# Where accumulating DMAs and transposes stand in the order of a hybrid encoder layer

## The chip, the cores and the metric

The kernel runs on one core of a Trainium2 chip. The metric is the device time of one execution in microseconds (us). Most executions of a kernel agree within 0.3%. The core has five engines, each with its own queue of instructions that it works off in order: TensorE (PE, matmuls, with its weight loads shown apart as PEld), VectorE (DVE), ScalarE (ACT), GpSimd (POOL) and SyncE (SP), which issues most of the DMA transfers. An instruction waits on semaphores for what other engines or transfers must finish first, and what is queued behind it on its engine waits with it.

## The reference

One layer of an encoder with two parallel groups of heads, for 256 tokens of 2048 features, in fp32:

```python
hn = _rmsnorm(h, norm_w[i])
proj = hn @ w_in[i]
q, v, f_fwd, f_bwd, z_a, b_gate, c_gate, h_b, z_b = jnp.split(proj, IN_SPLITS, axis=-1)
o_a = _hgrn2_bidirectional(jax.nn.silu(q), v, f_fwd, f_bwd, lb_all[:, i])
o_a = _head_rmsnorm(o_a, hgrn_norm_w[i]) * jax.nn.silu(z_a)
y_b = b_gate * _short_conv(c_gate * h_b, conv_w[i])
o_b = _rmsnorm(y_b, conv_norm_w[i]) * jax.nn.silu(z_b)
h = h + jnp.concatenate([o_a, o_b], axis=-1) @ w_out[i]
gate = jax.nn.sigmoid(h @ w_ple_gate[i])
h = h + (p[i] @ w_ple[i]) * gate
```

and a last RMSNorm. `_hgrn2_bidirectional` is a gated linear recurrence over 16 heads of 128 features, worked in chunks of 64 tokens, forward and backward: within a chunk masked scores times `v`, and between chunks a state of 128 x 128 for each head.

## The kernel before

**Tiles and precision.** Every fp32 operand of a matmul is split in two fp32r parts, a high and a low one, and products are made of three partial matmuls. `xs` holds the split activations. Weights come in raw tiles of up to 1 MB (`raw`, three buffers), loaded by SP. ACT casts a part of a tile to the high half of a `spl` tile (L101), DVE subtracts to get the low half (L102), and PE reads `spl`. There are five `spl` buffers; the split of a part is issued three parts ahead of its use.

**Stages.** Group A has 16 heads, worked as 8 pairs in four blocks of two pairs, called block 0, 2, 4 and 6 after the first pair (`two_pairs(i)`). A block has, for each of its pairs e = 0 and 1, three gemms of 16 k tiles: forward forget gate (FF), backward forget gate (FB) and Q, lines L403 (short matmuls, 256 columns) and L405 (long ones, 512 columns). Then `v` and `z_a` of both pairs follow: in block 0 as two gemms, in blocks 2, 4 and 6 together in `gemm_vz` (through `half`, lines L525 to L527) over eight pairs of k tiles. For three of these, k pairs 2, 4 and 6, seven products are made in place of eight, from sums and differences of the weights' blocks. These sums are made in DRAM: `prepare` copies the blocks (L306, DMAs of SP, "vz<-in_w_in_dram"), `add_up` accumulates into them with DMAs of POOL in three steps (step 0 on L314, two DMAs a sum; steps 1 and 2 on L318, one each), and then the weights' stream loads the result ("raw<-vz"). `w_out` has 16 such tiles of sums, four sets of four, 48 steps of `add_up` in all, worked off one by one by `pump()` (DMAs "sums<-in_w_out_dram", "sums<-sums"). Group B follows, 8 times the gemms CG, HB, BG and ZB with a convolution, then the gemms of `w_out`, of the gate and of the embedding, and a last norm.

**Mixing.** Behind the three gemms of a pair, `mix_forgets` scales `xf` and `qt` by the tokens' norms on POOL (L470), takes sigmoids on ACT (L592, L594) and logarithms (L601). `mix_pair` does scans and exponentials on DVE and ACT and makes `kc`, `qc` (L689) and `kx` (L695) on POOL. `scores` are PE's products (L708) and the cross-chunk part `cx` (L752), in the PSUM buffer "x"; POOL writes the masked scores `s` (L757). `outputs` makes the heads' outputs. In the block after, `gate_two` gates (`zt`, POOL L616), `finish_two` normalizes (`ogz`, DVE L626), and `turn` transposes a pair's outputs on PE (L636), one pair into the PSUM buffer "y" and one into "x", from which ACT (L639) and DVE (L640) write the split `mixa`. So `cx` of a block's first pair, in `gemm_vz`, uses the buffer "x" that the transpose of the previous block's second pair filled before.

**What sets the order.** The program is written out with `at(dt, fn)`: `fn` is issued `dt` k tiles later (`tick()` counts them and runs what is due; `gemm_vz` has 49 of them, every other gemm of 2 MB 16). The instructions of an engine then run in the order of the queue, with some splits and evacuations at a higher priority. In block i before the change: the `prepare`s at 0, 8 and 16; the nine `add_up`s and four `pump`s from tick 24 on every 6; `mix_forgets` behind each Q; scores of the first pair 4 ticks into `gemm_vz`; scores of the second pair 28 ticks and its outputs 40 ticks behind the end of `gemm_vz`, in the next block. `rest()` of a block runs behind the Q of the next block's first pair: gates at once, `finish_two` 30 ticks on, the transposes at 36 and 42. A gemm's `orders` ("kicks", `ONE` and `BOTH`) turn round the order of short and long matmuls at one or two k tiles.

The functions that the change touches, and what calls them:

Of the kernel before, what the change touches and what calls it, by code (L numbers as in the profile page):

```python
# [115 lines left out]
def tile_hymba_encoder(  # L116
# [34 lines left out]

    VZ_SUMS = (2, 4, 6)
    dramp = ctx.enter_context(tc.tile_pool(name="dramp", bufs=1, space=bass.MemoryType.DRAM))
    vz_prepared = {}
    blocks = {}
    for i in range(0, 8, 2):
# [4 lines left out]
        if i:  # L161
            blocks[B_V, i], vz_prepared[i] = [], []
            for q in range(8):
                srcs = [
                    [w_in[c + i + b, q // 4, :, 2 * (q % 4) : 2 * (q % 4) + 2] for b in range(2)] for c in (B_V, B_ZA)
                ]
                if q in VZ_SUMS:
                    sums = dramp.tile([P, 4, 512], F32, name=f"vz{i}_{q}")
                    vz_prepared[i].append((srcs, sums))
                    blocks[B_V, i].append(ws.add_sums(*srcs, sums))  # L170
                else:
                    blocks[B_V, i].append(ws.add(*srcs[0], *srcs[1]))
            continue
# [156 lines left out]
    def tick():  # L330
        now[0] += 1
        if now[0] in range(120, 160, 10):
            prepare(prepared[(now[0] - 120) // 10])
        due = sorted(e for e in pend if e[0] <= now[0])
        for e in due:
            pend.remove(e)
        for e in due:
            e[2]()
# [95 lines left out]
    def gemm_vz(i, vt, zt):  # L434
# [8 lines left out]
        main = [[acc[m], acc[2 + m]] for m in range(2)]  # L443
        for q1, q5, q6, q7 in half(main, extra, range(8), VZ_SUMS, blocks[B_V, i], xs, xq[0], True):
            d = xq[1][:, 0]
# [339 lines left out]
    def two_pairs(i):  # L785
# [4 lines left out]
        before = last_two[0]  # L790
        if i:

            todo = vz_prepared[i]
            for z, what in enumerate(todo):
                at(8 * z, lambda what=what: prepare(what))
            turns = [lambda what=what, step=step: add_up(what, step) for step in range(3) for what in todo]
            for j in (3, 7, 11, 12):
                turns.insert(j, pump)
            for j, fn in enumerate(turns):
                at(24 + 6 * j, fn)  # L800
        if i == 2:
# [9 lines left out]
        for e in range(2):  # L811
# [3 lines left out]

            kick = {(0, 1): ({}, ONE, BOTH)}.get((i, e), (ONE, BOTH, {}) if e == 0 else ({}, {}, {}))
            for j, (c, dst) in enumerate(((B_FF, xf[:, 0]), (B_FB, xf[:, 1]), (B_Q, qt))):
# [32 lines left out]
        else:  # L850
# [4 lines left out]
            at(12, lambda: out(0))  # L855
            at(28, lambda: steps[1][0]())
            at(40, lambda: out(1))

        def rest():
            gate_two(i, zt)  # L860
            if i < 6:
                at(30, lambda: finish_two(ogs, ss, zt, ogs))
                for e in range(2):
                    at(36 + 6 * e, lambda e=e: turn(i + e, ogs[e], "yx"[e]))
            else:
# [26 lines left out]
    for i in range(8):  # L892
        cg = ctmp.tile([P, 2, T], F32, tag="cg", name=f"cg{i}", bufs=2)
        evac(gemm_in(B_CG, i, {} if i else ONE), lambda m: cg[:, m, :], ctmp)
        hb = ctmp.tile([P, 2, T], F32, tag="hb", name=f"hb{i}", bufs=2)
        evac(gemm_in(B_HB, i, {} if i else BOTH), lambda m: hb[:, m, :], ctmp)
        u = ub[i % 2]
        by_norms(cg, rbc2, 2)
        pool.tensor_tensor(out=u[:, :, 1 : T + 1], in0=cg, in1=hb, op=ALU.mult)
        pump()  # L900
        for m in range(2):
            ct = 2 * i + m
            dve.tensor_scalar(cg[:, m, :], u[:, m, 0:T], cvw[:, 0, ct : ct + 1], None, op0=ALU.mult)
            for j in (1, 2):
# [3 lines left out]
                )  # L908
        evac(gemm_in(B_BG, i), lambda m: hb[:, m, :], ctmp)
        pool.tensor_tensor(out=cg, in0=cg, in1=hb, op=ALU.mult)  # L910
# [322 lines left out]
```

## Time and profile before

| | us |
|---|---|
| median of 3 runs | 1167.51 |
| lowest, highest | 1163.05, 1168.25 |
| the profiled execution | 1164.41 |
| its span | 1162.7 |
| mean granted TensorE clock | 0.981 of full speed |

| engine | busy us | share of the span |
|---|---|---|
| PE | 1111.8 | 96% |
| PE's weight loads | 951.6 | 82% |
| DVE | 825.8 | 71% |
| ACT | 681.5 | 59% |
| POOL | 300.4 | 26% |

The DMA engines moved 286.42 MB, 63.5% of their time for the queue that SP's transfers use and 15.3% for that of the accumulating DMAs. In the profile a line names an instruction's line in the kernel, its engine, the tile that it writes and those that it reads, partitions x elements, and a count. Idle time stands in brackets with the engine and tile that ended it. An idle engine costs something only where another, or the end, waits for it.

### The profile page before, as it was taken

The numbers are of one execution on the slowest core, as the hardware profiler recorded it, in microseconds if no ns is written. First come the engines' busy times: TensorE is split into PE (matmuls) and PEld (weight loads), VectorE is DVE, ScalarE is ACT, GpSimd is POOL, SyncE is SP. The second block draws the span as 40 slices with busy tenths as digits, with TensorE's granted clock in tenths as the row PEclk, the third lists the DMA queues.
The fourth block names the chain that finished last, engine by engine and source line by source line (L and its number), as shares of the span: only waits on it lengthen the run. The fifth ranks groups of instructions, "written<-read, shape, count | busy, mean of one in ns | idle before, by whom it ended". The sixth has DMA issues, their size and how long they took to land.

```text
span 1162.7 us, 17008 instructions
## 1 busy us (share of the span) xinstructions
PE 1111.8 (96%) x6455; PEld 951.6 (82%) x6455; DVE 825.8 (71%) x1100; ACT 681.5 (59%) x948; POOL 300.4 (26%) x251
## 2 busy tenths in 40 slices
PE   9999998899959999499999999999999999999996
PEld 8888887678858888388888888888888888888886
DVE  7899485875848676576666687686567879878573
ACT  7786475755945577565644445444446655565563
POOL 1135226513352036322323223223222000000001
PEclk9999999899979999799999999999999999999999
DMA  9757977799576998676789989989776988887531
GB/s 346 296 194 261 322 223 159 215 328 267 192 173 223 340 285 227 161 269 207 195 250 292 287 227 268 329 230 269 213 211 214 335 284 283 314 286 283 199 127 73
DMA packets 86082, 286.42 MB, mean 246 GB/s; under 512 B 8304, under 2 KB 29424, under 8 KB 67312
## 3 DMA queue, kind: packets, MB, share of 16 engines
q1 hardware_dynamic: 69264, 258.76, 63.5%
q0 software_dynamic: 16448, 26.22, 15.3%
q8 instruction: 51, 0.84, 0.3%
q10 hardware_dynamic: 288, 0.34, 0.1%
q14 instruction: 31, 0.25, 0.1%
HBM read 283.20 MB, written 54.53 MB: 290 GB/s over the span
## 4 chain that ended last, share of the span: by engine, by line
PE 70%; DVE 8%; POOL 7%; ACT 7%; DMA 5%; issue 3%; SPq 0%; DVEq 0%; ACTq 0%; POOLq 0%
PE a L405 26%; PE a L403 13%; DVE spl L102 4%; DMA raw<-in_w_in_dram 3%; PE pg L995 3%; PE pg L994 3%; PE pg L993 3%; ACT spl L101 2%; DMA vz<-vz 2%; PE pa L525 2%; PE pa L527 2%; PE pa L526 2%; POOL kc L689 2%; PE avz L526 1%; PE avz L525 1%
## 5 line engine op out<-in xcount | busy, mean ns | idle before, releaser
L102 DVE TENSOR_TENSOR spl<-raw,spl 128x1024 fp32r<-128x1024 f32 (+2 forms) x419 | 500.1, 1209 | 238.7 <-ACT spl L101 236.6
L405 PE MATMUL a<-xs,spl 128*128 128x512 f32 x1792 | 623.8, 395 | 2.6 <-DVE vt L455 2.4
L101 ACT CAST spl<-raw 128x1024 fp32r<-128x1024 f32 (+2 forms) x419 | 412.5, 998 | 268.2 <-PE a L403 120.5
L403 PE MATMUL a<-xs,spl 128*128 128x256 f32 x1792 | 494.4, 278 | 0.0
L405 PEld LDWEIGHTS a<-xs,spl 128*128 128x128 f32 x1792 | 335.2, 188 | 80.4 <-issue 3.2
L403 PEld LDWEIGHTS a<-xs,spl 128*128 128x128 f32 x1792 | 336.2, 188 | 2.2 <-DVE spl L102 0.6
L1110 POOL TENSOR_TENSOR hh<-hh,fw 128x512 f32<-128x512 f32 (+1 forms) x9 | 10.9, 1224 | 251.5 <-ACT gt L1109 248.8
L465 ACT COPY r<-a 128x256 f32<-128x256 f32 x112 | 40.5, 369 | 48.9 <-PE a L403 48.8
L526 PE MATMUL avz<-spl,xs 128*128 128x512 f32 x138 | 56.6, 410 | 0.7 <-DVE spl L102 0.7
L525 PE MATMUL avz<-spl,xs 128*128 128x512 f32 x138 | 56.8, 411 | 0.0
L527 PE MATMUL avz<-spl,xs 128*128 128x512 f32 x138 | 55.7, 404 | 0.0
L752 PE MATMUL cx<-qc,kx 128*128 128x128 f32 x64 | 11.9, 344 | 37.5 <-DVE mixa L640 36.5
L470 POOL TENSOR_TENSOR xf<-xf,rbc 128x1024 f32<-128x1024 f32 x8 | 28.1, 3518 | 66.9 <-DVE rbc L381 49.1
L993 PE MATMUL pg<-spl,ht 128*128 128x512 f32 (+1 forms) x120 | 45.2, 377 | 0.0
L994 PE MATMUL pg<-spl,ht 128*128 128x512 f32 (+1 forms) x120 | 45.1, 376 | 0.0
L995 PE MATMUL pg<-spl,ht 128*128 128x512 f32 (+1 forms) x120 | 45.0, 375 | 0.0
L752 PEld LDWEIGHTS cx<-qc,kx 128*128 128x128 f32 x64 | 10.2, 242 | 38.1 <-issue 36.7
L689 POOL TENSOR_TENSOR kc<-dd,ge 128x256 f32<-128x256 f32 x16 | 33.2, 2072 | 29.0 <-DVE dd L680 16.5
L101 ACT CAST spl<-early 128x1024 fp32r<-128x1024 f32 (+1 forms) x29 | 28.7, 990 | 20.0 <-PE pb_y L527 7.5
L102 DVE TENSOR_TENSOR spl<-early,spl 128x1024 fp32r<-128x1024 f32 (+1 forms) x29 | 33.0, 1148 | 9.7 <-ACT spl L101 9.1
L592 ACT ACTIVATE xf<-xf 128x1024 f32<-128x1024 f32 x8 | 8.5, 1060 | 45.1 <-POOL xf L470 45.0
L525 PE MATMUL pa<-spl,mixa 128*128 128x512 f32 x88 | 34.5, 392 | 0.0
(322 smaller groups left out, 1725.8 us busy)
## 6 DMA issues: line engine op xcount, KB each, us to landing
raw<-in_w_in_dram SPq DMA_DIRECT2D x106, 1024.0 KB, 7.4
raw<-in_w_in_dram SPq DMA_DIRECT2D x82, 256.0 KB, 4.3
raw<-in_w_out_dram SPq DMA_DIRECT2D x36, 512.0 KB, 5.3
sums<-in_w_out_dram SPq DMA_DIRECT2D x32, 512.0 KB, 9.9
raw<-in_w_in_dram SPq DMA_DIRECT2D x26, 512.0 KB, 5.2
raw<-sums SPq DMA_DIRECT2D x13, 1024.0 KB, 5.0
vz<-in_w_in_dram SPq DMA_DIRECT2D x36, 256.0 KB, 9.6
raw<-vz SPq DMA_DIRECT2D x9, 1024.0 KB, 5.2
```

Source lines behind the costliest of these rows:

```text
L101: self.nc.scalar.copy(out=v[:, :, 0], in_=r)
L102: self.nc.vector.tensor_tensor(out=v[:, :, 1], in0=r, in1=v[:, :, 0], op=ALU.subtract)
L403: pe.matmul(a[:, :T], lhsT=lhsT, rhs=xs[:, kt, 0, :], start=False, stop=(kt == NKT - 1))
L405: pe.matmul(a, lhsT=lhsT, rhs=xs[:, kt, :, :].rearrange("p s n -> p (s n)"), start=(kt == 0), stop=False)
L465: act.copy(out=r, in_=acc[m][:, 1, :])
L525: pe.matmul(acc, lhsT=ah, rhs=w[:, 0], start=start, stop=False)
L526: pe.matmul(acc, lhsT=ah, rhs=w[:, 1], start=False, stop=False)
L527: pe.matmul(acc, lhsT=al, rhs=w[:, 0], start=False, stop=stop)
L689: pool.tensor_tensor(out=c64(dst[:, d]), in0=c64(src[:, d, :, half * P : (half + 1) * P]), in1=g.unsqueeze(3).broadcast_to([P, 2, 2, CH]), ...
L993: pe.matmul(acc[m], lhsT=lh, rhs=wh, start=(kt == 0), stop=False)
L994: pe.matmul(acc[m], lhsT=lh, rhs=wl, start=False, stop=False)
L995: pe.matmul(acc[m], lhsT=ll, rhs=wh, start=False, stop=(kt == nk - 1))
```

## The change

1. The sums of `v`'s and `z_a`'s weights for a block are made in the block before: `prepare` at ticks 50, 60, 70 of block i for block i + 2, `add_up` at the ticks below.
2. All steps for `w_out`'s sums are done in group B, six `pump`s in each of the eight rounds; the first set's `prepare`s go from block 0 to block 6.
3. `gemm_vz` takes its k pairs in the order 0, 1, 2, 3, 4, 6, 5, 7.
4. `finish_two` at tick 24, both transposes at tick 32, between FB and Q of the block's second pair; the second scores at 32, the second outputs at 42.
5. The kicks are put at other gemms.

```diff
-    VZ_SUMS = (2, 4, 6)
+    VZ_ORDER, VZ_SUMS = (0, 1, 2, 3, 4, 6, 5, 7), (2, 4, 6)
...
-            for q in range(8):
+            for q in VZ_ORDER:
...
     def tick():
         now[0] += 1
-        if now[0] in range(120, 160, 10):
-            prepare(prepared[(now[0] - 120) // 10])
...
-        for q1, q5, q6, q7 in half(main, extra, range(8), VZ_SUMS, blocks[B_V, i], xs, xq[0], True):
+        for q1, q5, q6, q7 in half(main, extra, VZ_ORDER, VZ_SUMS, blocks[B_V, i], xs, xq[0], True):
...
-        if i:
-
-            todo = vz_prepared[i]
+        if i == 6:
+            for z in range(4):
+                at(10 + 10 * z, lambda z=z: prepare(prepared[z]))
+        else:
+
+
+            todo = vz_prepared[i + 2]
             for z, what in enumerate(todo):
-                at(8 * z, lambda what=what: prepare(what))
-            turns = [lambda what=what, step=step: add_up(what, step) for step in range(3) for what in todo]
-            for j in (3, 7, 11, 12):
-                turns.insert(j, pump)
-            for j, fn in enumerate(turns):
-                at(24 + 6 * j, fn)
+                at(50 + 10 * z, lambda what=what: prepare(what))
+                for step in range(3):
+                    dt = (126 + 10 * z, 160 + 4 * z, 174 + 4 * z)[step] if i else 98 + 6 * step + z
+                    at(dt, lambda what=what, step=step: add_up(what, step))
...
-            kick = {(0, 1): ({}, ONE, BOTH)}.get((i, e), (ONE, BOTH, {}) if e == 0 else ({}, {}, {}))
+            kicks = {(0, 1): ({}, ONE, BOTH), (2, 0): (ONE, BOTH, {}), (4, 0): ({}, {}, BOTH), (6, 0): ({}, {}, BOTH)}
+            kick = kicks.get((i, e), ({}, {}, BOTH if i + e else {}))
...
-            at(28, lambda: steps[1][0]())
-            at(40, lambda: out(1))
+            at(32, lambda: steps[1][0]())
+            at(42, lambda: out(1))
...
-                at(30, lambda: finish_two(ogs, ss, zt, ogs))
+                at(24, lambda: finish_two(ogs, ss, zt, ogs))
                 for e in range(2):
-                    at(36 + 6 * e, lambda e=e: turn(i + e, ogs[e], "yx"[e]))
+                    at(32, lambda e=e: turn(i + e, ogs[e], "yx"[e]))
...
-        evac(gemm_in(B_CG, i, {} if i else ONE), lambda m: cg[:, m, :], ctmp)
+        evac(gemm_in(B_CG, i), lambda m: cg[:, m, :], ctmp)
...
-        evac(gemm_in(B_HB, i, {} if i else BOTH), lambda m: hb[:, m, :], ctmp)
+        evac(gemm_in(B_HB, i), lambda m: hb[:, m, :], ctmp)
...
         by_norms(cg, rbc2, 2)
+        pump()
...
-        evac(gemm_in(B_BG, i), lambda m: hb[:, m, :], ctmp)
+        evac(gemm_in(B_BG, i, {} if i else BOTH), lambda m: hb[:, m, :], ctmp)
```

How this moves instructions shows in the queues. The first place is POOL in block 2, from `kx` of the first pair to `xf` of the second (`vz_2`, `vz_4`, `vz_6` are the sums of the three k pairs, `sums_0_3` to `sums_0_5` tiles for `w_out`). Before:

```order
L695 TENSOR_TENSOR kx_1707<-kc_1701,ge_1688 128x512
L318 DMA vz_4_82<-vz_4_82 128x512
L318 DMA vz_6_83<-vz_6_83 128x512
L314 DMA sums_0_3_91<-in_w_out_dram 256x1x512
L318 DMA vz_2_81<-vz_2_81 128x512
L318 DMA vz_4_82<-vz_4_82 128x512
L318 DMA vz_6_83<-vz_6_83 128x512
L314 DMA sums_0_4_92<-in_w_out_dram 256x1x512
L314 DMA sums_0_5_93<-in_w_out_dram 256x1x512
L470 TENSOR_TENSOR xf_1709<-xf_1709,rbc 128x1024
```

And the same place in the changed kernel (lines count two less here), on through `gemm_vz`, with the next block's sums:

```order
L693 TENSOR_TENSOR kx_1703<-kc_1697,ge_1684 128x512
L468 TENSOR_TENSOR xf_1705<-xf_1705,rbc 128x1024
L468 TENSOR_TENSOR qt_1706<-qt_1706,rbc 128x512
L755 TENSOR_TENSOR s_2104<-early 128x256 x2
L314 DMA vz_2_84<-in_w_in_dram 256x1x256
L593 TENSOR_TENSOR qt_1706<-qt_1706,sq_2020 128x512
L314 DMA vz_2_84<-in_w_in_dram 256x1x256
L314 DMA vz_4_85<-in_w_in_dram 256x1x256 x2
L314 DMA vz_6_86<-in_w_in_dram 256x1x256 x2
L318 DMA vz_2_84<-vz_2_84 128x512
L318 DMA vz_4_85<-vz_4_85 128x512
```

The eight DMAs between `kx` and `xf` are gone from there; eight others now stand behind the first pair's `s`, within `gemm_vz`.

The second place is ACT in block 2, around the transposes' `mixa` of the previous block and the table load of the second pair's sigmoid (`spl65` to `spl67` are parts of weights). Before:

```order
L465 COPY r_1899<-a24_3_1_1802 128x256
L101 CAST spl65_1957<-raw32_1933 128x1024
L639 ACTIVATE mixa_499<-ogt0_1923,vec_108 128x256 x2
L101 CAST spl66_1991<-raw33_1986 128x1024
L639 ACTIVATE mixa_499<-ogt1_1968,vec_108 128x256
L592 ACT_TABLE_LOAD
L592 ACTIVATE xf3_1709<-xf3_1709 128x1024
L101 CAST spl67_2036<-raw33_1986 128x1024
L639 ACTIVATE mixa_499<-ogt1_1968,vec_108 128x256
```

And changed:

```order
L463 COPY r_1920<-a24_3_1_1804 128x256
L637 ACTIVATE mixa_499<-ogt0_1899,vec_108 128x256
L637 ACTIVATE mixa_499<-ogt1_1908,vec_108 128x256
L637 ACTIVATE mixa_499<-ogt0_1899,vec_108 128x256
L637 ACTIVATE mixa_499<-ogt1_1908,vec_108 128x256
L101 CAST spl65_1968<-raw32_1944 128x1024
L590 ACT_TABLE_LOAD
L590 ACTIVATE xf3_1705<-xf3_1705 128x1024
```

All four `mixa` now stand ahead of the table load and of a cast, where the last stood behind the sigmoid before.

The third place is POOL early in block 4, from `kx` of block 2's second pair to its `s`, in the changed kernel:

```order
L693 TENSOR_TENSOR kx_2476<-kc_2470,ge_2457 128x512
L687 TENSOR_TENSOR qc_2471<-pf_2447,ge_2457 128x256
L318 DMA vz_6_86<-vz_6_86 128x512
L318 DMA vz_2_84<-vz_2_84 128x512
L318 DMA vz_4_85<-vz_4_85 128x512
L318 DMA vz_6_86<-vz_6_86 128x512
L755 TENSOR_TENSOR s_2671<-early 128x256
L468 TENSOR_TENSOR xf_2401<-xf_2401,rbc 128x1024
L755 TENSOR_TENSOR s_2671<-early 128x256
```

The last four accumulating DMAs of block 4's sums stand there, ahead of `s`; before, the first two of the twelve (L314, `vz_2`) stood between this `kx` and `s`, and the others behind.

## The prediction

> **What bounds the kernel now.** I read the page's busy times first, then PE's waits, then the stretch ahead of the longest waits engine by engine, then the DMA.
>
> ```profile
> span 1162.7 us, 17008 instructions
> PE 1111.8 (96%) x6455; PEld 951.6 (82%) x6455; DVE 825.8 (71%) x1100; ACT 681.5 (59%) x948; POOL 300.4 (26%) x251
> L752 PE MATMUL cx<-qc,kx 128*128 128x128 f32 x64 | 11.9, 344 | 37.5 <-DVE mixa L640 36.5
> ```
>
> PE is busy for 96% of the span, so only three things shorten the kernel: PE's idle time, matmuls that run slowly, or fewer matmuls. The change leaves the matmuls as they are, so the first two are left. One line, `cx`, the first matmuls of a pair's scores, carries 37.5 us of idle time. PE's waits say how it is spread:
>
> ```profile
> PE cx L752 <- DVE mixa L640: 36.5, 3, 15.5
> PE a L405 <- DVE vt L455: 2.4, 2, 1.2
> PE avz L526 <- DVE spl L102: 0.7, 1, 0.7
> ```
>
> Three waits, the longest of 15.5 us, one in each of blocks 2, 4 and 6. `cx` takes the PSUM buffer "x", which the second transpose of the previous block filled and which DVE's `mixa` line frees. Why is `mixa` late? First POOL in block 4 (start, duration, instruction, idle time before it with its releaser), then ACT and PE:
>
> ```profile
> 322.70 1.05 POOL L695 TENSOR_TENSOR kx<-kc,ge 128x512 f32<-128x512 f32 x1
> 323.69 1.66 POOL L318 DMA_DIRECT2D vz<-vz  x2
> ...
> 328.82 0.81 POOL L318 DMA_DIRECT2D vz<-vz  x1 [1.80 <-DMA vz<-vz]
> 331.46 0.81 POOL L318 DMA_DIRECT2D vz<-vz  x1 [1.82 <-DMA vz<-vz]
> ...
> 333.05 3.26 POOL L470 TENSOR_TENSOR xf<-xf,rbc 128x1024 f32<-128x1024 f32 x1
> ```
>
> ```profile
> 324.07 1.28 ACT L592 ACT_TABLE_LOAD   x1
> 336.34 1.06 ACT L592 ACTIVATE xf<-xf 128x1024 f32<-128x1024 f32 x1 [10.98 <-POOL xf L470]
> 338.24 0.47 ACT L639 ACTIVATE mixa<-ogt,vec 128x256 fp32r<-128x256 f32 x1
> 341.99 0.48 ACT L639 ACTIVATE mixa<-ogt,vec 128x256 fp32r<-128x256 f32 x1
> ```
>
> ```profile
> 323.08 0.60 PE L636 MATMUL ogt<-ident,ogz 128*128 128x128 f32 x4
> 344.01 2.05 PE L752 MATMUL cx<-qc,kx 128*128 128x128 f32 x8 [12.10 <-DVE mixa L640]
> ```
>
> The chain reads backwards. POOL has `kx` done at 323.75. Its queue then holds accumulating DMAs, several of which wait for an earlier one to land, so `xf` starts only at 333.05. ACT sits 10.98 us on `xf`'s sigmoid with its table loaded, and behind it in its queue stand the second transpose's two `mixa`. PE did that transpose at 323.08, but ACT copies it out at 338.24 and 341.99, DVE's `mixa` line follows, and PE has stood for 12.10 us when `cx` starts.
>
> The stall also slows what follows it. PEclk, the seventh column here (after the busy times of five engines and before DMA share and GB/s), is the granted clock in the 6 us from each `cx`:
>
> ```profile
> 208.25:214.25 6.00, 6.00 (x20) 5.10 (x21) 5.58 (x10) 5.92 (x8) 2.52 (x3) 0.56 1.03 327
> 344.01:350.01 6.00, 6.00 (x18) 5.13 (x19) 6.00 (x8) 3.06 (x4) 4.24 (x4) 0.50 0.12 43
> 480.65:486.65 6.00, 6.00 (x18) 5.13 (x19) 6.00 (x8) 3.05 (x4) 4.23 (x4) 0.50 0.20 73
> ```
>
> Lost there: 6.00 x (0.44 + 0.50 + 0.50) = 8.6 us.
>
> **The change, part by part.** The sum is made against the profiled execution, 1164.4 us (span 1162.7 and 1.7 around it); the median of the runs shown, 1167.5, lies 3.1 above it. I don't add those 3.1, since the landing times in the stalls are a likely part of what varies.
>
> *The stall.* Behind block 4's `kx` POOL's order now has `xf` and `qt` at once: no accumulating DMA stands between. By the rows, `xf` can start at 323.75 instead of 333.05 and end by 327.0. On ACT all four `mixa` now stand ahead of the table load and the sigmoid, and both transposes are issued together at the end of FB, 16 k tiles of Q ahead of `v`/`z_a`. So the buffer is free long before `cx` asks for it: all 36.5 us go, and the 8.6 with them. What could be late next is the transposes' own input, which PE would wait for ahead of Q:
>
> ```profile
> 314.33 0.61 DVE L626 SCALAR_TENSOR_TENSOR ogz<-ogz,ss,zt 128x128 f32<-128x128 f32 x2
> ...
> 449.20 0.61 DVE L626 SCALAR_TENSOR_TENSOR ogz<-ogz,ss,zt 128x128 f32<-128x128 f32 x2
> ```
> ```profile
> 315.70 0.39 PE L405 MATMUL a<-xs,spl 128*128 128x512 f32 x1
> 318.48 0.60 PE L636 MATMUL ogt<-ident,ogz 128*128 128x128 f32 x4
> ...
> 451.67 0.60 PE L636 MATMUL ogt<-ident,ogz 128*128 128x128 f32 x4
> ```
>
> In block 4 `ogz` is complete at 314.94 and Q begins at 315.70, so it would be in time by 0.8 us. In block 6 it is complete at 449.81; Q begins 2.8 us (318.48 - 315.70) ahead of the transpose, at 448.9, so PE would wait 0.9 us. The gating's start moves six k tiles earlier, but in the rows `ogz` is paced by POOL's and ACT's gates, so I don't count that as a gain: +1.0 for block 6, bounds 0 and 3 (1 us in each block).
>
> *Order of the sums in `v`/`z_a`* (the sum for k pair 6 ahead of plain pair 5). The DVE work on the last sum no longer stands at the very end, where `a <- vt` waited 2.4 us: -2.0, bounds -2.4 and 0. Against it, four loads now follow one another faster. Block 4 shows how little slack there is now:
>
> ```profile
> 367.31 3.47 ACT L101 CAST spl<-raw 128x1024 fp32r<-128x1024 f32 x4 [2.52 <-DMA raw<-in_w_in_dram]
> ```
> ```profile
> 368.39 4.14 DVE L102 TENSOR_TENSOR spl<-raw,spl 128x1024 fp32r<-128x1024 f32 x4 [1.30 <-ACT spl L101]
> ```
> ```profile
> 371.02 0.39 PE L525 MATMUL avz<-spl,xs 128*128 128x512 f32 x1
> ```
>
> ACT already waits for the DMA there. The first of the four splits ends near 369.6 (368.39 and some 1.2), PE uses it at 371.02: 1.4 us to spare.
>
> *The accumulating DMAs.* Those of the next block's sums are now issued within `v`/`z_a` and early in the block after. What this does to the weight loads shows where the old order let them meet (issue, engine, operation, count, KB each, median us to landing; the first fence 190 to 216 us, with adds in flight, the second 360 to 370 us, without):
>
> ```profile
> vz<-vz POOLq DMA_DIRECT2D x5, 256.0 KB, 7.6
> raw<-vz SPq DMA_DIRECT2D x1, 1024.0 KB, 9.1
> raw<-in_w_in_dram SPq DMA_DIRECT2D x4, 256.0 KB, 6.8
> ```
> ```profile
> raw<-in_w_in_dram SPq DMA_DIRECT2D x6, 256.0 KB, 4.3
> raw<-vz SPq DMA_DIRECT2D x1, 1024.0 KB, 5.2
> ```
>
> A load of sums is 3.9 us later (9.1 against 5.2), a piece of plain weights 2.5 (6.8 against 4.3). With 1.4 us to spare, a load hit makes PE late by 1.1 to 2.5 us. Blocks 2 and 4 issue adds within `v`/`z_a`; block 6 does not. Bounds for a block: 0 (adds land in the plain first half), and 11.4 with all four late loads hit (2 x 2.5 + 2 x 3.9 - 1.4). I take one hit a block, 2 us, as the adds are spread by POOL's own work: +4.0 for the two, 0 to 23. [...]
>
> *`w_out`'s sums.* Twelve of 48 add-up steps go from group A to group B:
>
> ```profile
> 560.00:960.00 400.00, 400.00 (x2216) 346.54 (x2215) 278.91 (x372) 208.35 (x278) 97.03 (x82) 1.00 0.87 261
> q0 software_dynamic: 16448, 26.22, 15.3%
> ```
>
> In group B PE has no gap, while the DMA engines have 13% of 400 us free, 52 us. The adds' queue took 15.3% of 1162.7 us for 26.22 MB, 6.8 us per MB; 12 steps of 0.5 MB, 41 us, fit. Cost 0. [...]
>
> *Kicks* (which of the short and long matmuls of a k tile comes first, in other gemms than before) and the scores' and outputs' ticks move 4 and 2 k tiles, with the same instructions. The order within a pair of matmuls can move a gemm by little; 0, bounds -2 and +2, my estimate from the pace of a gemm, 24 of its long matmuls in 8.40 us in one order and 25 in another:
>
> ```profile
> 277.65:286.05 8.40, 8.40 (x24) 4.46 (x24) 1.00 0.85 186
> 300.00:308.40 8.40, 8.40 (x25) 4.58 (x25) 1.00 0.47 165
> ```
>
> **Sum:** 1164.4 - 36.5 - 8.6 - 2.0 + 4.0 + 1.0 = **1122.3 us**.
>
> **Rivals.**
>
> *The weights become the wait.* The two sums side by side need their loads in quick succession while adds share the DMA engines. For it: 1.4 us to spare, and 9.1 against 5.2. Against it: PE waited for splits 0.7 us in all so far, and an add is in flight for only part of the gemm. Three of four late loads hit: 2.5 + 2.5 + 3.9 - 1.4 = 7.5 a block, 15 for two, in place of the 4.0: 1122.3 - 4.0 + 15 = 1133 (1126 to 1140).
>
> *Only part of the stall goes.* Four `mixa` now come together on ACT and DVE; if DVE's queue of splits holds them up, `cx` waits again, or Q waits for "y" and "x". For it: DVE is busy in 5.58 to 6.00 of 6 us in the windows above. Against it: 16 k tiles of Q lie between. With half of the 45.1 us left: 1122.3 + 22.5 = 1145.
>
> *Slower: the adds hold up the second scores.* POOL's order puts four accumulating DMAs between `kx` of a block's second pair and the copy `s` that its outputs wait for, the later ones waiting for the earlier to land.
>
> ```profile
> 233.17 1.05 POOL L695 TENSOR_TENSOR kx<-kc,ge 128x512 f32<-128x512 f32 x1
> 277.17 2.51 POOL L757 TENSOR_TENSOR s<-early 128x256 f32<-128x256 f32 x2 [21.76 <-DVE early L756]
> vz<-vz POOLq DMA_DIRECT2D x1, 256.0 KB, 18.1
> ```
>
> From 234.2 to 277.2 there are 43 us for them. At the usual 7.6 us four in a row take 30. At the longest landing of the trace, 18.1 us, they take 72, so `s` comes 29 us late and PE stops at the outputs, in two places: 58, against the 47.1 gained (36.5 + 8.6 + 2.0): 1164.4 + 58 - 47.1 = 1175. It decides where a landing takes more than 43 / 4 = 10.8 us throughout. Against it: only single ones took that long, and three sums let the adds overlap.
>
> **How the numbers follow.** Forecast 1122.3 with its own range 1112 to 1130: 0.62. Weights, 1133: 0.25. Part of the stall, 1145: 0.08. Slower, 1175: 0.03; about no change, as where two of these meet: 0.02. The low end is no late load, no wait at the transposes and the kicks' -2: 1164.4 - 36.5 - 8.6 - 2.4 - 2 = 1115, less 3 for the spread of the runs: 1112. The high end takes in most of the weights' case: 1137. A measurement of this kernel tells 0.5%, 5.8 us, from no change. Faster by more: 0.95; within: 0.02; slower: 0.03.
>
> **What would show it.** Right: `cx <- mixa` gone from PE's waits, POOL's `xf` following `kx` within 1 us in blocks 2 to 6, ACT's four `mixa` ahead of the sigmoid's table load, and a granted clock of 1.00 through the first 6 us of each `v`/`z_a`. The term for the weights shows as `avz <- spl` waits of about 4 us in all (rival: over 10), with `raw` landing later than 5.2 us in blocks 2 and 4. It is wrong if PE waits at the transposes (`ogt <- ogz`), at `s` or the outputs, if group B gets gaps, or if more than 10 us of new idle time stand on a line that had none.

## The result and the profile after

The changed kernel takes 1153.87 us (median of 4 runs, 1151.24 to 1155.43) against 1165.33 us before (4 runs, 1163.05 to 1168.25). The ratio is 0.9898, with a 95% interval of 0.9861 to 0.9935. It is faster by 1%; the forecast was 1122.3 us, outside whose range of 1112 to 1137 it lies. The profiled execution of the change took 1151.24 us, its span is 1149.5.

The busy times and PE's waits of the changed kernel (us in total, times, longest):

```profile
span 1149.5 us, 17024 instructions
PE 1114.5 (97%) x6455; PEld 950.8 (83%) x6455; DVE 829.3 (72%) x1100; ACT 677.6 (59%) x947; POOL 300.3 (26%) x251
```
```profile
PE ey L523 <- ACT spl L101: 9.8, 5, 3.1
PE avz L524 <- DVE spl L102: 5.0, 6, 2.0
PE ey L524 <- DVE spl L102: 3.8, 5, 0.8
PE ex L524 <- DVE spl L102: 3.2, 3, 1.4
PE avz L523 <- DVE qt L464: 1.2, 1, 1.2
...
PE ex L523 <- ACT spl L101: 0.4, 1, 0.4
...
PE a L403 <- DVE vt L453: 0.2, 1, 0.2
```

The 36.5 us of `cx <- mixa` are gone. In their place stand 22.2 us (9.8 + 5.0 + 3.8 + 3.2 + 0.4) of waits for split weights in `v`/`z_a`: 9.3 in block 2, 9.7 in block 4 and 3.2 in block 6. From the first matmul of `v`/`z_a` to the first of the next gemm, in the three blocks that work both together:

| | block 2 | block 4 | block 6 |
|---|---|---|---|
| before, us | 58.5 | 59.2 | 64.0 |
| changed, us | 61.3 | 59.5 | 48.4 |

Block 6 has what was forecast in kind. Blocks 2 and 4 take as long as before or longer, and these two are the ones with accumulating DMAs in `v`/`z_a`. So one kernel holds both cases. The DMA issues of the changed kernel from 330 to 390 us (block 4), and then from 463 to 512 us (block 6; count, KB each, median us to landing):

```profile
raw<-in_w_in_dram SPq DMA_DIRECT2D x16, 256.0 KB, 8.7
...
raw<-vz SPq DMA_DIRECT2D x2, 1024.0 KB, 13.5
...
vz<-in_w_in_dram POOLq DMA_DIRECT2D x6, 256.0 KB, 9.2
vz<-vz POOLq DMA_DIRECT2D x6, 256.0 KB, 9.8
```
```profile
raw<-in_w_in_dram SPq DMA_DIRECT2D x16, 256.0 KB, 5.0
...
raw<-vz SPq DMA_DIRECT2D x2, 1024.0 KB, 6.4
```

Beside the adds a load of sums takes 13.5 us in place of 6.4, a piece of plain weights 8.7 in place of 5.0. POOL's queue in block 4 of the change shows when the adds ran (start, duration, instruction, idle time before and what ended it):

```profile
340.23 5.79 POOL L314 DMA_DIRECT2D vz<-in_w_in_dram  x5
...
351.92 0.82 POOL L318 DMA_DIRECT2D vz<-vz  x1 [4.43 <-DVE spl L102]
...
358.33 0.82 POOL L318 DMA_DIRECT2D vz<-vz  x1 [2.09 <-DMA vz<-in_w_in_dram]
360.90 0.83 POOL L318 DMA_DIRECT2D vz<-vz  x1 [1.76 <-DMA vz<-vz]
...
368.37 0.81 POOL L318 DMA_DIRECT2D vz<-vz  x1 [4.68 <-DMA vz<-vz]
```

`v`/`z_a` runs from 330.3 to 389.8 there. All twelve adds ran within it, the first (one more L314, at 338.4) 8 us behind its start and the last 38 us behind it. By their ticks, 160 to 182, the six L318 belong to the next block, and four of them stand behind the second pair's `kx` in the order. A tick gives a place in POOL's queue, not a time: POOL had nothing else to wait for between that `kx` and the next block's `s`, so it issued them as soon as their inputs had landed.

The waits also bring back the half clock: 0.50 for 3.41 us each from 230.63, 240.87, 363.75 and 373.99 us on. Two windows of the change, one in block 2 and one in block 4 (columns as in the prediction):

```profile
225.00:245.00 20.00, 13.65 (x40) 8.68 (x38) 7.18 (x8) 7.17 (x9) 3.27 (x4) 0.83 1.05 277
360.00:380.00 20.00, 12.88 (x38) 9.28 (x39) 8.74 (x8) 8.68 (x10) 2.45 (x3) 0.83 1.02 280
```

At most 20 x 0.17 = 3.4 us are lost in each, 6.8 in all, since PE also waits for 6.4 and 7.1 us within them. The DMA share is 1.05 and 1.02: the DMA engines are full.

### The profile page after: what moved, and what is told of

The parts are those of the page before. It is cut to its first block, busy times and chain, and to the rows that moved or that the text cites. A ratio compares the mean times of both kernels' runs of the same rounds, so it can differ in the third digit from the quotient of the medians.

```text
span 1149.5 us, 17024 instructions
## 1 busy us (share of the span) xinstructions
PE 1114.5 (97%) x6455; PEld 950.8 (83%) x6455; DVE 829.3 (72%) x1100; ACT 677.6 (59%) x947; POOL 300.3 (26%) x251
## 4 chain that ended last, share of the span: by engine, by line
PE 70%; DVE 11%; DMA 6%; POOL 6%; ACT 4%; issue 2%; SPq 0%; DVEq 0%; ACTq 0%; POOLq 0%
PE a L403 28%; PE a L401 14%; DVE spl L102 4%; DMA raw<-in_w_in_dram 4%; PE pg L996 3%; PE pg L997 3%; PE pg L995 3%; DMA raw<-vz 2%; PE pa L523 2%; PE pa L524 2%; PE pa L525 2%; ACT spl L101 2%; POOL kc L687 2%; DVE pf L652 1%; POOL qc L687 1%
## 5 line engine op out<-in xcount | busy, mean ns | idle before, releaser
L524 PE MATMUL avz<-spl,xs 128*128 128x512 f32 x138 | 55.4, 401 | 4.9 <-DVE spl L102 4.8
L523 PE MATMUL avz<-spl,xs 128*128 128x512 f32 x138 | 55.3, 401 | 1.2 <-DVE qt L464 1.2
L525 PE MATMUL avz<-spl,xs 128*128 128x512 f32 x138 | 54.5, 395 | 0.0
L755 POOL TENSOR_TENSOR s<-early 128x256 f32<-128x256 f32 x16 | 16.3, 1028 | 105.4 <-DVE early L754 105.4
L468 POOL TENSOR_TENSOR xf<-xf,rbc 128x1024 f32<-128x1024 f32 x8 | 20.8, 2602 | 68.7 <-DVE rbc L379 49.3
L524 PEld LDWEIGHTS avz<-spl,xs 128*128 128x128 f32 x138 | 26.5, 192 | 12.8 <-DVE spl L102 7.5
L912 POOL TENSOR_TENSOR cg<-cg,hb 128x512 f32<-128x512 f32 x8 | 14.8, 1854 | 82.1 <-DVE hb L464 82.1
L523 PE MATMUL pa<-spl,mixa 128*128 128x512 f32 x88 | 34.5, 392 | 0.0
L525 PE MATMUL pa<-spl,mixa 128*128 128x512 f32 x88 | 34.3, 390 | 0.0
```

The costliest lines, as they stand in the source:

```text
L523: pe.matmul(acc, lhsT=ah, rhs=w[:, 0], start=start, stop=False)
L524: pe.matmul(acc, lhsT=ah, rhs=w[:, 1], start=False, stop=False)
L525: pe.matmul(acc, lhsT=al, rhs=w[:, 0], start=False, stop=stop)
```

## The experiments

Theory A: the adds in flight beside the weights' loads make PE wait in `v`/`z_a`; B: the weights can't keep up once the stall no longer gives them time, adds or not. The medians, the ratios to the kernel before on the same chip, and the three lengths of `v`/`z_a` in the profiled execution of each. The runs come from several chips, on which the kernel before has medians of 1161.0 to 1165.3 us, so a small difference between two rows is read by the ratios as well as by the medians:

| run | median, us | ratio, 95% interval | `v`/`z_a`, us |
|---|---|---|---|
| change | 1153.87 | 0.9898 (0.9861 to 0.9935) | 61.3, 59.5, 48.4 |
| e1_turns | 1157.74 | 0.9962 (0.9930 to 0.9994) | 56.7, 56.2, 59.9 |
| e2_noadds | 1129.89 | 0.9700 (0.9637 to 0.9764) | 50.1, 48.5, 48.8 |
| e3_order | 1151.37 | 0.9883 (0.9825 to 0.9940) | 60.6, 55.0, 48.9 |
| e4_spread | 1161.26 | 0.9978 (0.9952 to 1.0004) | 65.8, 56.5, 50.3 |
| e5_gaps | 1139.97 | 0.9809 (0.9789 to 0.9829) | 54.7, 48.3, 48.8 |
| e6_oldturns | 1136.38 | 0.9782 (0.9765 to 0.9799) | 51.7, 50.8, 50.6 |
| e7_step0 | 1138.86 | 0.9803 (0.9786 to 0.9820) | 56.2, 52.2, 47.2 |
| e8_gaps_order | 1140.75 | 0.9807 (0.9784 to 0.9831) | 54.5, 48.9, 49.2 |
| e9_gaps2 | 1138.61 | 0.9796 (0.9762 to 0.9829) | 49.1, 48.0, 48.6 |
| e10_late_mix | 1139.21 | 0.9801 (0.9763 to 0.9839) | 50.9, 48.3, 48.4 |
| e11_gaps3 | 1142.59 | 0.9825 (0.9796 to 0.9853) | 53.5, 53.9, 48.4 |
| e12_fewer_scans | 1127.26 | 0.9714 (0.9678 to 0.9749) | 49.1, 47.1, 47.0 |
| e13_gaps4 | 1127.69 | 0.9713 (0.9685 to 0.9740) | 50.5, 48.2, 48.0 |

### The transposes alone

```diff
 # the kernel before
-                at(30, lambda: finish_two(ogs, ss, zt, ogs))
+                at(24, lambda: finish_two(ogs, ss, zt, ogs))
-                    at(36 + 6 * e, lambda e=e: turn(i + e, ogs[e], "yx"[e]))
+                    at(32, lambda e=e: turn(i + e, ogs[e], "yx"[e]))
```

> The kernel before with one part of the change alone: the normalizing at tick 24 and both transposes at tick 32; the sums, the kicks and the order of k pairs stay as before. Theory A (in the change, accumulating DMAs in flight beside the weights' loads in v/z_a of blocks 2 and 4 make PE wait for splits; the stall at cx itself came from the transposes' place): cx <- mixa vanishes from PE's waits, no adds run in the second half of v/z_a, so 36.5 + 8.6 us of 1165 go and some 3 us of waits for splits come: 1120 to 1128 us. Theory B (the weights can't keep up with v/z_a once the stalls no longer give them time, adds or not): waits for splits of 20 us and more, 1140 us or above. A middle way: POOL's late xf still holds ACT for 11 us and with it casts of weights, PE waits for splits in the first quarter of v/z_a: 1130 to 1140.

1157.74 us: by the number it lies in theory B's range (1140 or above), but the waits are not for splits, as B has it. `cx` no longer waits for `mixa`; something right behind it does. PE's longest wait, and ACT in block 4 of this run:

```profile
PE avz L525 <- DVE qt L466: 29.2, 3, 11.5
```
```profile
332.05 1.06 ACT L592 ACTIVATE xf<-xf 128x1024 f32<-128x1024 f32 x1 [9.14 <-POOL xf L470]
...
336.79 0.64 ACT L465 COPY r<-a 128x256 f32<-128x256 f32 x2
```

ACT still stands 9.14 us at `xf`'s sigmoid, since POOL's adds are still ahead of `xf`. Behind it now stands the copy that empties Q's PSUM tiles (L465, then DVE's L466 for `qt`), and `v`/`z_a` needs those. The stall has only changed its victim: 36.5 us at one line, 29.2 at the next.

### Without the adds for blocks 4 and 6

```diff
 # the changed kernel
-                for step in range(3):
+                for step in range(0 if i else 3):
```

> The changed kernel without the accumulating DMAs for the sums of blocks 4 and 6 (24 of 256 KB; the copies stay, so these sums hold only their first term and the output is not the reference's). Theory A: v/z_a of blocks 2 and 4 take as long as block 6's, whose 48.5 us in the change had no adds beside it, in place of 61.4 and 59.5: 1151 - 24 = 1127, range 1124 to 1131, and raw<-vz lands in 5 to 7 us there in place of 13. Theory B, or if the order of the k pairs alone makes the waits: above 1143 us.

1129.89 us, as theory A said, 24.0 less than the change; the three lengths are 50.1, 48.5 and 48.8. The DMA issues in block 4's `v`/`z_a`, and PE's waits that are left:

```profile
raw<-in_w_in_dram SPq DMA_DIRECT2D x16, 256.0 KB, 4.5
...
raw<-vz SPq DMA_DIRECT2D x2, 1024.0 KB, 6.3
```
```profile
PE avz L524 <- DVE spl L102: 6.4, 3, 2.3
...
PE avz L523 <- DVE qt L464: 1.1, 1, 1.1
...
PE ey L524 <- DVE spl L102: 0.9, 2, 0.5
```

So the weights mostly keep up without the stalls (7.3 us of waits for splits are left), and theory B falls. 24 adds of 256 KB cost 24.0 us by the medians, 23 by the ratios (0.9898 - 0.9700 of some 1161 us), in the places where the change puts them.

### The old order of the k pairs

```diff
 # the changed kernel
-    VZ_ORDER, VZ_SUMS = (0, 1, 2, 3, 4, 6, 5, 7), (2, 4, 6)
+    VZ_ORDER, VZ_SUMS = (0, 1, 2, 3, 4, 5, 6, 7), (2, 4, 6)
```

> The changed kernel with the k pairs of v/z_a in the old order, 0 to 7, so that no two sums stand side by side. Theory A: the adds stay, so nearly all waits stay: within 5 us of the change, 1149 to 1159. The rival, that the two sums side by side need their loads too quickly: some 20 us of the waits go, 1130 to 1136.

1151.37 us: within the bounds for theory A, and its interval overlaps the change's. Two sums side by side are not what makes the 24 us; whether they add to it is open, since block 4's `v`/`z_a` was 4.5 us shorter in the one profiled execution. The order does what the prediction said at the end of `v`/`z_a` (`a <- vt` waits 2.4 us again in this run, 0.2 in the change), but the time doesn't show it.

### Part of the adds

```diff
 # the changed kernel
-                for step in range(3):
+                for step in range(1 if i else 3):
```

> The changed kernel with step 0 of the adds for blocks 4 and 6 and without their steps 1 and 2 (the sums are not complete, so the output is not the reference's): six accumulating DMAs of 256 KB in each of v/z_a of blocks 2 and 4, issued from 10 to 17 us behind its start, and none later. Theory A, by count: half of the 24 us between 1153.9 and 1129.9 stays, 1138 to 1146. If only adds in flight in the second half, where three of the four loads of sums lie, cost time: 1130 to 1135.

1138.86 us: within theory A's 1138 to 1146, and not the other reading's 1130 to 1135. By the medians half the adds (step 0) cost 9 of the 24 us (1138.86 - 1129.89); by the ratios it is 12 of 23 (0.9803 - 0.9700), and by the lengths of `v`/`z_a` in blocks 2 and 4 it is 9.8 of 22.2. So adds in the first half cost time too, and the cost goes roughly with the count; whether those of the second half cost more is not shown.

### The old transposes without adds

```diff
 # the run without the adds
-                at(24, lambda: finish_two(ogs, ss, zt, ogs))
+                at(30, lambda: finish_two(ogs, ss, zt, ogs))
-                    at(32, lambda e=e: turn(i + e, ogs[e], "yx"[e]))
+                    at(36 + 6 * e, lambda e=e: turn(i + e, ogs[e], "yx"[e]))
```

> The run without the adds for blocks 4 and 6, with the normalizing and the transposes at their old ticks, 30, 36 and 42. If the adds ahead of xf made the stall at cx, then POOL's xf comes early here as well, ACT's sigmoid doesn't hold the transposes' mixa up, and cx waits little: 1129.9 to 1134 us. If the transposes' place made it, cx waits for mixa by several us in each block: 1137 or above.

1136.38 us, 6.5 more than with the new places (9.5 by the ratios), with

```profile
PE cx L750 <- DVE mixa L638: 9.4, 3, 3.6
```

in its waits: between the two readings. With the first run this makes a square: with adds ahead of `xf`, the new places bring 0.4% (0.9962); without, 0.6 to 0.8%. Adds ahead of `xf` made most of the stall, since 9.4 of its 36.5 us stay without them; the transposes' place made the rest.

### Other places for the adds

```diff
 # e4_spread, against the changed kernel
-                at(50 + 10 * z, lambda what=what: prepare(what))
+                at((8 if i else 50) + 10 * z, lambda what=what: prepare(what))
-                    dt = (126 + 10 * z, 160 + 4 * z, 174 + 4 * z)[step] if i else 98 + 6 * step + z
+                    dt = (81 + 2 * z, 188 + z, 205 + 2 * z)[step] if i else 98 + 6 * step + z
```

> The changed kernel with the adds for blocks 4 and 6 elsewhere: copies at ticks 8, 18, 28 of the block before, step 0 behind that block's kx of the first pair, steps 1 and 2 in the own block behind the second scores and behind kx. Theory A: only one or two adds are left in v/z_a, its length in blocks 2 and 4 falls to 48 to 51 us: 1127 to 1134. If the six to eight adds ahead of xf hold up ACT's sigmoid and with it weights' casts, up to 9 us a block come back: 1138 to 1146. Theory B: no gain on the change, above 1146.

1161.26 us, as slow as before. Six to eight adds stood ahead of the second pair's `xf` again, and `avz <- qt` waited 18.2 us, as in the first run: the second reading, and more than its price. So neither place will do, beside `v`/`z_a`'s loads or ahead of `xf`. The next run uses the time in which POOL is idle and nothing is queued closely behind: between its `xf` and `qt` of the first pair, and behind the gates `zt`.

```diff
 # e5_gaps, against the changed kernel
         by_norms(xf.rearrange("p a b t -> p (a b) t"), rbc, 4)
+        if between:
+            between()
...
+        behind_xf = {2: [(4, 0)], 4: [(4, 2), (6, 0)], 6: [(6, 2)]}.get(i, [])
+        behind_zt = {2: [(4, 1)], 4: [(6, 1)]}.get(i, [])
...
                     if before:
                         before()
+                    adds(*behind_zt)
```

Here `(4, 0)` is step 0 of block 4's three sums, `between` the list `behind_xf` for the first pair; block 4's copies stand at ticks 118, 126 and 134 of block 0, block 6's at 50 to 70 of block 2.

> The changed kernel with the adds for blocks 4 and 6 where POOL has nothing else to do and nothing waits behind them: step 0 between POOL's xf and qt of the first pair one block ahead, step 1 behind that block's gates (zt), step 2 between xf and qt of the own block; copies for block 4 in block 0, for block 6 in block 2. Theory A (adds cost time only beside the weights' loads of v/z_a or ahead of the second pair's xf): as without the adds, 1129.9, plus up to 6 us for loads of the plain gemms: 1128 to 1136. Rival: adds cost their DMA time wherever they stand, so that the plain gemms wait for splits instead: 1145 or above, with a <- spl in PE's waits.

1139.97 us: faster than both kernels, and with all work done, but above the 1128 to 1136 expected and below the rival's 1145. Blocks 4 and 6 are as without adds (48.3 and 48.8). What is left lies in block 2 and in the gemms just ahead of its `v`/`z_a`; only 1.3 of the first line's 5.5 us are there, the other 4.2 in blocks 4 and 6, where the run without adds has such waits too:

```profile
PE avz L524 <- DVE spl L102: 5.5, 4, 2.2
PE avz L523 <- DVE qt L464: 3.6, 1, 3.6
PE a L401 <- DVE spl L102: 2.4, 3, 1.1
PE a L403 <- ACT spl L101: 1.4, 2, 0.7
```

with copies that land in 11 to 22 us between 120 and 155 us, where block 2's adds run as well. Three further spreads follow. In the first, block 4's copies stand at ticks 100 to 116, block 6's at 0 to 16 of block 4, and step 0 of block 2's sums behind `xf` of block 0's second pair:

```diff
 # e9_gaps2, against e5_gaps
-                at(118 + 8 * z, lambda what=what: prepare(what))
+                at(100 + 8 * z, lambda what=what: prepare(what))
...
-                at(50 + 10 * z, lambda what=what: prepare(what))
+                at(8 * z, lambda what=what: prepare(what))
...
+        behind_xf1 = {0: [(2, 0)]}.get(i, [])
```

> The run with the adds in POOL's gaps, with less of DMA at one time in block 0 and early block 2, where it still waited (some 10 us behind the run without adds, all of it in block 2): step 0 of block 2's sums behind POOL's xf of block 0's second pair, copies for block 4 at ticks 100, 108 and 116 of block 0, copies for block 6 at 0, 8 and 16 of block 4. Theory A: the waits a <- spl and avz <- qt of block 2 go: 1130 to 1136 us. If the copies and adds cost their DMA time wherever they stand: 1139 to 1143, the waits only in other places.

1138.61 us, close to the second reading's 1139 to 1143. Block 2's step 0 came ahead of its copies here, so that its sums lack their second term; the traffic is the same. The waits of block 2 did go (`v`/`z_a` 49.1), and others came in block 0 instead, as that reading says:

```profile
PE a L422 <- ACT spl L101: 4.5, 1, 4.5
PE a L423 <- DVE spl L102: 1.5, 2, 1.0
```

```diff
 # e11_gaps3, against e5_gaps
-        behind_xf = {2: [(4, 0)], 4: [(4, 2), (6, 0)], 6: [(6, 2)]}.get(i, [])
-        behind_zt = {2: [(4, 1)], 4: [(6, 1)]}.get(i, [])
+        behind_xf = {4: [(4, 1), (6, 0)], 6: [(6, 2)]}.get(i, [])
+        behind_zt = {2: [(4, 0)], 4: [(4, 2), (6, 1)]}.get(i, [])
```

Copies for block 4 stand at ticks 16 to 32 of block 2, for block 6 at 0 to 16 of block 4.

> The changed kernel with the adds in POOL's gaps, in a third spread that takes copies and adds out of block 0 and the start of block 2, where the DMA engines were full: copies for block 4 at ticks 16 to 32 of block 2, for block 6 at 0 to 16 of block 4; step 0 for block 4 behind the gates (zt) of block 2, the other steps between xf and qt or behind the gates of blocks 4 and 6. Theory A: no place is left where adds meet full DMA engines and a tight consumer, so that the time comes to that of the run without adds, 1129.9 us: 1129 to 1134, ratio to the kernel before 0.970 to 0.976. If adds cost their DMA time wherever they stand: 1137 to 1142 as in the two spreads before.

1142.59 us, a miss. The wait of the first run is back, for 8.0 us, in two ways. In block 2 the six adds behind the gates delay `kx` and with it `xf`, which starts 2.1 us ahead of `v`/`z_a` in place of 5.5 in the change. In block 4 `xf` is not late, but the six adds issued there from 309.3 us on are in flight until 327.4, pieces of weights take 9.8 us (median) beside them, and ACT's cast of one, which stands ahead of the copy that `qt` needs, waits 3.49 us for its load:

```profile
PE avz L523 <- DVE qt L464: 8.0, 2, 4.7
```

By now each spread had crowded block 0's end, held up `xf` or met the loads for `v`/`z_a`. The last one avoids all three: block 4's copies at ticks 79 to 91 of block 0, block 6's at 0 to 16 of block 4.

```diff
 # e13_gaps4, against e5_gaps
-                at(118 + 8 * z, lambda what=what: prepare(what))
+                at(79 + 6 * z, lambda what=what: prepare(what))
...
-                at(50 + 10 * z, lambda what=what: prepare(what))
+                at(8 * z, lambda what=what: prepare(what))
```

> As the first run with the adds in POOL's gaps, but the copies for block 4 stand at ticks 79, 85 and 91 of block 0 (ahead of block 2's adds in time) and those for block 6 at 0, 8 and 16 of block 4, so that copies and adds no longer meet between 112 and 175 us. All work is done. Theory A (adds and copies cost time only where the DMA engines are full beside a tight consumer, or ahead of xf): the waits of block 2 go, 1130 to 1135, ratio to the kernel before 0.971 to 0.977. If they cost their time wherever they stand: 1137 to 1142, with waits for splits in block 0 instead.

1127.69 us (5 runs, 1126.77 to 1128.69), ratio 0.9713 (0.9685 to 0.9740): the fastest with all work done, a little under the 1130 to 1135 expected, and with an interval that overlaps that of the run without the adds (0.9637 to 0.9764). PE's waits, POOL in block 4 of this run, and the loads of sums in its `v`/`z_a`:

```profile
PE avz L524 <- DVE spl L102: 6.5, 3, 2.3
PE avz L523 <- DVE qt L464: 1.7, 1, 1.7
```
```profile
276.01 2.50 POOL L318 DMA_DIRECT2D vz<-vz  x3
277.61 7.25 POOL L314 DMA_DIRECT2D vz<-in_w_in_dram  x6
289.92 2.20 POOL L468 TENSOR_TENSOR qt<-qt,rbc 128x512 f32<-128x512 f32 x1 [5.07 <-DVE qt L464]
...
301.00 2.53 POOL L318 DMA_DIRECT2D vz<-vz  x3
```
```profile
raw<-vz SPq DMA_DIRECT2D x2, 1024.0 KB, 6.6
```

Nine adds are issued between `xf` and `qt`, and POOL still waits 5.07 us for `qt` behind them; the loads of sums take 6.6 us again. So the 24 us were the price of the adds' place, not of the adds. One thing was not tried: the copies in these new places without the adds, which could be faster than the run without adds was.

### The order of the k pairs once more

```diff
 # e5_gaps
-    VZ_ORDER, VZ_SUMS = (0, 1, 2, 3, 4, 6, 5, 7), (2, 4, 6)
+    VZ_ORDER, VZ_SUMS = (0, 1, 2, 3, 4, 5, 6, 7), (2, 4, 6)
```

> The run with the adds in POOL's gaps, with the k pairs of v/z_a in the old order, 0 to 7. If the waits a <- vt at the end of v/z_a (2.4 us before) are what the order changes: 2 us slower than the other. If two sums side by side cost more than that in loads: up to 3 us faster.

1140.75 against 1139.97 us, with intervals that nearly coincide: no difference that can be told here either, though `a <- vt` waits 3.6 us in this run.

### What is left: DVE's scans

```diff
 # e9_gaps2
-            at(8, lambda: steps.append(mix_pair(i + 1, *forgets[1])))
+            at(20, lambda: steps.append(mix_pair(i + 1, *forgets[1])))
```

> As the run beside it (adds in POOL's gaps, spread), with mix_pair of the second pair issued 20 in place of 8 ticks behind the end of v/z_a's program order, so that DVE's scans come later. Theory: the wait of 2.0 to 2.3 us in each of v/z_a of blocks 2, 4 and 6 (avz <- DVE spl), with half clock behind it, is DVE's burst of scans ahead of the splits; it goes or moves: 3 to 9 us faster than the run beside it. If the order of DVE is not what makes it: no difference, within 2 us.

1139.21 us, and it tells nothing of the question: the order of DVE's instructions came out the same as without the edit, so that it is a second run of e9_gaps2 (block 2's sums lack a term here too). The next one takes work away:

```diff
 # e2_noadds
         for h in range(2):
+            if h and i in (3, 5, 7):
+                for d in range(2):
+                    dve.memset(pv[d][:, h, :], -0.5)
+                continue
             dve.tensor_tensor_scan(
```

> The run without the adds for blocks 4 and 6, and without two of the four scans of mix_pair for the second pair of blocks 2, 4 and 6 (a memset in their place, so the output is not the reference's): some 3 us less of DVE work in the first third of v/z_a. What is tested is the wait of 2.0 to 2.3 us there (avz <- DVE spl) that remains without adds. If DVE's scans ahead of the splits make it, it goes, and the half clock behind it: 6 to 10 us less than 1129.9, that is 1120 to 1124, ratio 0.962 to 0.966. If the splits are late for their loads or casts: 1127 or above.

1127.26 us: by its number the second reading (1127 or above), and its interval (0.9678 to 0.9749) overlaps that of the run without adds. In the profiles the place tested does change: the waits there fall from 6.4 us to

```profile
PE avz L524 <- DVE spl L102: 2.9, 3, 1.2
```

and the half clock behind them goes. But `ey`, later in the same gemm, now waits 4.3 us for splits (2.3 and 2.0) in place of 0.9, so that PE waits as long for splits in all, 7.2 against 7.3 us. The same stretch of block 4 without the adds, first with all scans, then with half of them:

```profile
337.00:343.00 6.00, 3.97 (x12) 2.83 (x11) 6.00 (x5) 3.70 (x5) 5.45 (x4) 0.78 0.42 164
```
```profile
337.00:343.00 6.00, 5.13 (x23) 4.03 (x22) 6.00 (x5) 2.81 (x4) 3.50 (x3) 1.00 0.42 143
```

The three lengths are 1.0, 1.4 and 1.8 us shorter, some 4 us in one execution of each. DVE is busy for all of the 6 us in both: its scans stand ahead of the splits, and they make the long wait at this place. What they cost in time these runs don't settle.

## Why the prediction was wrong

**Right: the chain of the stall.** `xf` follows `kx` at once, and the 36.5 us of `cx <- mixa` are gone with the 8.6 us of half clock behind them: the granted clock is 1.00 from 196 to 208, from 330 to 342 and from 464 to 476 us. POOL in block 4 of the change:

```profile
323.03 1.05 POOL L693 TENSOR_TENSOR kx<-kc,ge 128x512 f32<-128x512 f32 x1
324.04 2.40 POOL L468 TENSOR_TENSOR xf<-xf,rbc 128x1024 f32<-128x1024 f32 x1
```

But of the prediction's two reasons, adds and transposes, it gave no shares. The runs do: the transposes alone bring 0.4%; and with the adds gone from POOL's queue there, all but 9.4 us of the stall goes even with the old transposes. What was "late next" was also not only `ogz`: `qt`'s evacuation stands behind the same sigmoid. That cost the change only 1.2 us.

**Wrong: the term for the accumulating DMAs, +4.0.** It measured 24.0 us (1153.87 - 1129.89; 23 by the ratios), six times the term and at the upper end of 23 that it was given. Of the 31.6 us by which the forecast was off, 20.0 stand here. Three things in that step failed. First, when the adds run: the prediction read "within `v`/`z_a` and early in the block after" from ticks and queue places, and all twelve ran within. Had it followed POOL's queue in time, as it did for the stall, it would have seen that POOL is idle from `kx` on (the 21.76 us before `s` are in a row it quoted) and runs ahead. Second, how many loads are hit: one of four was taken; with adds in flight through most of `v`/`z_a`, all loads of its second half came late. Third, what a late load costs: 13.5 us against 6.4, where the row used, with adds that met it in part, had 9.1 against 5.2; and the new waits halve the clock again, at most 6.8 us in the two windows above, which the step left out though it had just priced the same thing for the old stall.

The loads of sums took 6.4 us in block 6 of the change, with no adds beside them, and 13.0 and 13.5 us in blocks 2 and 4, with adds: about twice as long. The prediction's row without adds had 5.2 us, so it had the load without adds too low as well.

**Put at nothing: the waits for splits that the stall had hidden.** Without adds for blocks 4 and 6 the kernel is at 1129.9, while the sum without its 4.0 is 1118.3. Of the 11.6 us between, 8.4 are idle time that the trace names: 7.3 for splits (6.4 + 0.9) and 1.1 for `qt`. Before, PE waited 0.7 us for splits. The three long waits are DVE's scans ahead of the splits, by the run with half of them; what DVE's work costs in all is not shown, since shorter waits took their place there. In the old stall's windows, quoted in the prediction, DVE was busy for 5.58 to 6.00 of 6.00 us, read there only as a point for a rival. The rest of the 11.6 stays open. The half clock is no ready answer: one execution of the run without adds had a mean clock of 0.997 and took 1129.26 us, the three at 0.993 and 0.994 took 1129.60 to 1130.91, about 1 us more, where 0.004 of 1128 us would be 4.5.

**The sum over again.** From the profiled 1164.4: -36.5, -8.6, -2.2 for `a <- vt`, +22.2 for splits, +6.8 at most for the clock, +1.2 for `qt` make 1147.3. The change's profiled time is 1151.2; the 3.9 between were not followed further.

**Small terms.** The waits at the end of `v`/`z_a` went from 2.4 to 0.2 us (forecast -2.0), but two pairs of runs show no difference in time from the order. PE didn't wait at the transposes (+1.0 forecast). `w_out`'s sums in group B cost nothing, as forecast: its gemms took 361.3 us before and 361.1 in the change, while the DMA share rose:

```profile
525.00:886.30 361.30, 361.30 (x2167) 316.21 (x2168) 240.96 (x323) 180.80 (x253) 102.85 (x87) 1.00 0.84 246
```
```profile
512.10:873.20 361.10, 361.10 (x2168) 318.42 (x2168) 244.52 (x322) 178.40 (x254) 119.06 (x97) 1.00 0.92 267
```

The kicks were not tried apart from the rest; the stretch of group B, in which some of them were moved, shows no cost.

**The rivals.** "The weights become the wait" named the mechanism, but at 1133 with three of four late loads a block; the kernel ended 21 us higher. The slower rival didn't come: no wait for `s` or the outputs appears, though the four adds ahead of `s` were the ones that ran beside the loads. The range ended at 1137 because the term and this rival were priced from the same rows.

## What to carry to other kernels

A place in an in-order queue is not a time: here four adds that the ticks put into the next block ran 28 to 38 us into this block's `v`/`z_a`, where POOL waited only for earlier adds to land (1.14 to 4.68 us each). So follow the moved instruction through the idle time of its own queue and see which transfers it will meet. Work moved out of the way of one wait has to be given a place by what is scarce there: here a queue with nothing closely behind, and DMA engines that are not full beside a tight consumer; the same 24 DMAs cost some 24 us in one place and nothing measurable in another. A long stall also hides other engines' lateness, here 8.4 us of waits for splits and `qt` in the run without adds, so price what each of them still has to do in that stretch before the whole stall is counted as gain.

## What the runs showed of the hardware

The granted clock falls behind far shorter waits than the stalls of 8.9 to 15.5 us, but not behind each of them. PE starts again behind a wait for a split in block 4 of the run without adds, at the same place of the run with half of the scans, and in block 6 of the change:

```profile
340.11 0.58 PE L524 MATMUL avz<-spl,xs 128*128 128x512 f32 x1 [2.03 <-DVE spl L102]
```
```profile
338.16 0.50 PE L524 MATMUL avz<-spl,xs 128*128 128x512 f32 x1 [0.86 <-DVE spl L102]
```
```profile
484.12 0.50 PE L524 MATMUL avz<-spl,xs 128*128 128x512 f32 x1 [2.03 <-DVE spl L102]
```

Behind 0.86 us the clock stays at 1.00, in the window quoted for the scans. The two waits of 2.03 us end differently, the first with half clock, the other without (columns as before):

```profile
336.99:340.40 3.41, 1.38 (x6) 0.85 (x5) 3.41 (x4) 2.67 (x4) 3.33 (x3) 1.00 0.74 288
340.40:343.81 3.41, 3.41 (x9) 2.64 (x9) 3.41 (x3) 1.04 (x1) 2.13 (x2) 0.50 0.14 45
```
```profile
479.80:483.21 3.41, 2.29 (x11) 1.55 (x9) 3.41 (x5) 3.41 (x5) 2.71 (x4) 1.00 0.76 255
483.21:486.62 3.41, 2.50 (x11) 2.06 (x12) 3.41 (x3) 1.50 (x2) 3.33 (x2) 1.00 0.25 103
```

In these rows PE idled for 2.03 us (3.41 - 1.38) in the 3.41 us ahead of the half clock, which lasted for 3.41 us; the other wait lies partly in each of its two rows, with 1.12 and 0.91 us of idle time (3.41 - 2.29 and 3.41 - 2.50), and the clock stayed at 1.00 in both. So two waits of the same length ended differently.

But for the last microseconds of each trace, the clock is at half four times for 3.41 us in the change, and for 10.24, 13.65 and 17.07 us in the kernel before, from 203.33, 336.45 and 469.57 us on. In the 3.41 us ahead of these seven stretches PE idled for 1.63, 2.40, 2.72 and 2.91 us in the change and for all 3.41 us, three times, in the kernel before.
